# ScalarE's order in a two-FFN decoder step: one copy moved ahead, one cast moved behind, and two loads swapped

## The chip, the cores and the metric

One core of a Trainium2 chip runs the whole step in one launch. The metric is the device time in microseconds; three runs of the kernel before gave a median of 1117.8 us (1117.29 to 1119.15).

Engine names as in the profile: PE is TensorE (matmul), PEld its weight load, DVE is VectorE, ACT is ScalarE, POOL is GpSimd, SP is SyncE, which here only issues DMA loads.

## The reference

One inference step of one decoder layer, in float32, for 512 prompt tokens and 8 x 8 sample tokens, which the kernel treats as 576 columns of one matrix `x`:

```python
x = x + 0.5 * swiglu(rmsnorm(x, ffn1_norm), w_gate, w_up, w_down)   # 1024 -> 2816 -> 1024
h = rmsnorm(x, mix_norm); proj = h @ w_in                          # RG-LRU heads and pooling heads
x = x + concat(y_lru, y_pool) @ w_out
x = x + cross_attend(rmsnorm(x, xattn_norm), mem_k, mem_v, wq, wo)  # 4 heads, 256 memory tokens
x = x + 0.5 * swiglu(rmsnorm(x, ffn2_norm), ...)
y = rmsnorm(x, final_norm)                                         # plus new states, keys and values
```

Prompt tokens attend to keys computed here; each group of sample tokens has its own cached keys (`cache_mem_k`).

## The kernel before

**Arithmetic.** Every operand of a large matmul is kept as two parts: `split` makes a high part with an ACT cast and the low part, the rest, with a DVE subtraction (`wh_`/`wl_` for weights, `dh`/`dl` for weights of the way down, `ph`/`pl` for hidden values). A product is three matmuls: high by high, high by low, low by high.

The larger part of both FFNs, and the query projection, use a scheme with seven block products in place of eight. Weights and activations are cut in 2 x 2 blocks; the products are called 11, E, 22, F, G, 12 and H after the weight block or sum of blocks that they use, and T1 to T4 are sums of activation blocks ("the fourth sum" is T4). The weights come from HBM raw; DVE and POOL's accumulating DMAs form the sums, and `parts_of` or `prepare_22` splits them. `prepare_g` forms the sums for G and F and casts both with one instruction: this is *block G's cast*, `wh_g`.

**The loop of an FFN.** In `ffn`, the loop over `f` handles one chunk of 128 hidden columns: products 11, E, (product 22 of the chunk before, in `finish_chunk`), F, G, 12, H, each of 12 matmuls of 288 columns. Two of these products share a PSUM bank `U`: 11 starts it and F adds to it; then H adds, and 22. Between them ACT must have copied the bank: `out_[0] = s.copy(u2, U)` behind F is *block F's copy*. `u2` goes into the gate, `g`, then Silu (L860) and the up part, `e`; from pairs of chunks `build_a` and `build_b` make the hidden operand (in `build_b`, for odd chunks, the fourth sum's cast).

**The way down.** For the first 16 chunks the product with `w_down` uses the same scheme, in `quick`: for each group of four chunks (`f` = 4, 8, 12, 16) four times the six steps s11, sE, sF, s12, sH and (sG, s22), each of 6 matmuls. These steps are put between the products of the loop: `fill()` stands at seven places in each chunk and runs one step. So the 24 steps of a group run through the chunks with a shift: the fill just behind block F's copy runs s11 in chunks 4, 8, 12, 16, sE in the next chunk, sF in the one after, s12 in the fourth. Each step's result is copied out of PSUM by ACT: s11 and sF with `s.copy` into the banks A (L643, `dA<-dU`) and D (L658, `dD<-dU`), the others with `take` (L636, `add<-...`), which halves it for an accumulating DMA on POOL into `x`. `taken[0]` is the last of these. `ensure` prepares the step's weights (`td` to `dh`, `dl`), `fetch_pair` loads them.

**The order.** PE runs the matmuls as written. On every other engine a planner sets the order when the kernel is built, from the program's order, its own estimate of each duration, and the free buffers. `after_(i, j)` adds an edge without a semaphore: `i` is placed behind `j`. Every engine, and each DMA queue, then runs in its fixed order: what waits holds up all behind it.

**Buffers.** Raw weights use six buffers of one tag, `wr`; a load on SP waits until a buffer's last reader is done. High and low parts have four each, `dh` and `dl` three each.

**The query stage.** `query(p)`, for p = 0 to 3, runs the seven products for two of the eight 128-column blocks of q. In between, `sample_scores(j)` multiplies the sample queries with the cached keys, loaded by `load_keys(j)` (two loads of 512 KB into `wr`), and `load_q(p)` loads raw query weights (also two of 512 KB), used by `prepare_q`, whose additions POOL does for p > 0. Before, `query(p)` calls `load_q(p + 2)` first, and `load_keys(2 * p - 2)` behind `sample_scores(2 * p - 1)`; the scores of block 2p - 2 follow later in the same query.

Of the kernel before, what the change touches and what calls it, by code (L numbers as in the profile page):

```python
# [11 lines left out]
AF = mybir.ActivationFunctionType  # L12
# [57 lines left out]
def hybrid_step(ctx, tc, a):  # L70
# [70 lines left out]
    def after_(i, j):  # L141

        tc.add_manual_dep(i.ins, j.ins.name, mybir.DependencyInfo(
            mybir.DependencyClass.NoSync, mybir.DependencyReason.DATA), reason="order")
# [43 lines left out]
    def split(hi, lo, src, scale=None):  # L188

        if scale is None:  # L190
            i = cast[0] = s.copy(hi, src)  # L191
            if first[0] is not None:
                after_(i, first[0])
            return v.tensor_tensor(out=lo, in0=src, in1=f(hi), op=ALU.subtract)  # L194
        s.activation(hi, src, AF.Copy, scale=scale)
        return v.scalar_tensor_tensor(out=lo, in0=src, scalar=scale, in1=f(hi), op0=ALU.mult, op1=ALU.subtract)
# [171 lines left out]
    def ffn(name, n, fp, turn, plain, head=False):  # L368
# [53 lines left out]
        def parts_of(src, nm_):  # L422
            w = [wp.tile([P, 2, KP, P], F32R, tag=tag, name=f"{tag}_{nm_}") for tag in ("wh", "wl")]
            split(*w, src)
            if out_[0] is not None and nm_ == "e":
                after_(cast[0], out_[0])
            return [lambda q, k, i=i: w[q][:, i, k, :] for i in range(2)]
# [34 lines left out]
        def prepare_g(f):  # L462
            if f < FFC:
                r0, r1 = raws[f]
                v.tensor_add(r0[:, 1], r0[:, 1], r0[:, 0])
                v.tensor_add(r0[:, 0], r0[:, 1], r1[:, 0])  # L466
                W[f]["G"], W[f]["F"] = parts_of(r0, "g")

        def prepare_h(f):
            if f < FFC:  # L470
# [91 lines left out]
        def build_b(p):  # L562
            (hi, lo), b2 = pairs[p], raw[2 * p + 1]
            b21 = b2[:, :HT]
            split(hi[:, N21:N22 + 1, :], lo[:, N21:N22 + 1, :], halves(b2), -1.0)
            v.tensor_sub(b21, b21, t2[p])  # L566
            split(hi[:, T4, :], lo[:, T4, :], b21)

        def build_plain(f):
            if f // 2 not in pairs:  # L570
# [1 line left out]
            split(*hidden(f), raw[f])  # L572

        draw, dparts, made, taken = {}, {}, [0], [None]

        td = fp.tile([P, 4, 2, P], F32, name="td")

# [46 lines left out]
        def quick(g):  # L624

            ps = {}

            def put(i, nm_, b, out, start):
                w = dparts.pop((i, nm_))
                for k in range(2):  # L630
                    for m, (qw, qx) in enumerate(((0, 0), (0, 1), (1, 0))):
                        mm(out, lhsT=w[qw][:, k, :], rhs=pairs[2 * g + k][qx][:, b, :],
                           start=start and k == 0 and m == 0, stop=k == 1 and m == 2, skip_group_check=True)

            def take(dst, src, sign):
                taken[0] = s.activation(dst, src, AF.Copy, scale=0.5 * sign)  # L636

            def s11(i):
                ensure(4 * i + 2)
                ps[i] = cols([single("d", q) for q in ("dU", "dC", "dA", "dD")])  # L640
                U, C, A, D = ps[i]
                put(i, "11", N11, U, True)
                s.copy(A, U)  # L643

            def sE(i):
                U, C, A, D = ps[i]
                put(i, "E", T1, C, True)
                t = halves(rows.tile([P, T], F32, tag="acc", bufs=1, name="add_e"))
                take(t[:, 0, :], C, -1)
                take(t[:, 1, :], C, 1)  # L650
                j = 2 * (i % NQ)
                nc.gpsimd.dma_start(x[:, j:j + 2, HT:], t, accum_op=ALU.add)  # L652

            def sF(i):
                ensure(4 * i + 3)
                U, C, A, D = ps[i]
                put(i, "F", T2, U, False)
                s.copy(D, U)  # L658

            def s12(i):  # L660
                U, C, A, D = ps[i]
                put(i, "12", N21, A, False)
                ps[i, 1] = rows.tile([P, T], F32, tag="sq", name="add_1")
                take(ps[i, 1][:, :HT], A, -1)

            def sH(i):
                ensure(4 * i + 4)
                U, C, A, D = ps[i]
                put(i, "H", T3, U, False)
                ps[i, 2] = rows.tile([P, T], F32, tag="sq", name="add_2")  # L670
                take(ps[i, 2][:, HT:], U, 1)

            def sG(i):
                ensure(4 * i + 5)
                U, C, A, D = ps[i]
                put(i, "G", N22, D, False)
                t = ps.pop((i, 1))
                take(t[:, HT:], D, -1)
                nc.gpsimd.dma_start(x[:, 2 * (i % NQ), :], t, accum_op=ALU.add)  # L679

            def s22(i):
                U, C, A, D = ps[i]
                put(i, "22", T4, U, False)
                t = ps.pop((i, 2))
                take(t[:, :HT], U, 1)
                nc.gpsimd.dma_start(x[:, 2 * (i % NQ) + 1, :], t, accum_op=ALU.add)  # L686

            for i in range(g * NQ, (g + 1) * NQ):
                steps.extend([(q, i) for q in qs] for qs in ((s11,), (sE,), (sF,), (s12,), (sH,), (sG, s22)))
# [121 lines left out]
        for f in range(plain, FFC):  # L811
            w = W[f]
            U, C, A = (single(tag, f"p{tag}")[:, :HT] for tag in "uca")
            product(U, w["11"], n, N11, True)
            out_[0] = s.copy(A, U)
            if f == plain:
                if not head:
                    prepare_g(f)
                load_11(f + 2)
            if f == FFC - 5:  # L820
                fetch(0)
            fill()
            product(C, w["E"], n, T1, True)
            e1 = small_tile("e1")
            out_[0] = s.copy(e1, C)  # L825
            prepare_h(f)
            load_12(f + 2)
            if f == plain:
                sum_eh(f + 1)
            if f == 3:  # L830
                build_a(0)
                build_b(0)
            fill()
            if before:
                finish_chunk(before)
                raw[f - 1] = before[2]
                build(f - 1)
            if f == PLAIN[1][0]:
                down(0)
            prepare_e(f + 1)  # L840
            fill()
            if f in range(4, 4 * FAST + 1, 4):
                quick(f // 4 - 1)
            product(U, w["F"], n, T2, False)
            u2 = small_tile("u2")
            out_[0] = s.copy(u2, U)
            prepare_22(f)
            load_22(f + 2)
            fill()
            product(C, w["G"], n, N22, False)  # L850
            g = full_tile("g")
            v.tensor_add(g[:, HT:], C, u2)
            v.tensor_mul(g[:, HT:], g[:, HT:], r[:, HT:])
            sum_eh(f + 2)
            fill()
            if f == plain:
                (n.last if head else n.last_split)(0, ts[0][:, :, 0, :])
            product(A, w["12"], n, N21, False)
            v.tensor_mul(g[:, :HT], A, r[:, :HT])  # L859
            silu = s.activation(g, g, AF.Silu, scale=-1.0)  # L860
            v.tensor_mul(g, g, r)
            fill()
            if taken[0] is not None:
                after_(silu, taken[0])
            product(U, w["H"], n, T3, False)
            v.tensor_add(e1, U, e1)
            v.tensor_mul(g[:, HT:], e1, g[:, HT:])
            if f == plain:
                (n.last if head else n.last_split)(1, ts[1][:, :, 0, :])
            prepare_g(f + 1)  # L870
            load_11(f + 3)
            raw[f] = g
            if f % 2 and f < 4 * FAST:
                build_a(f // 2)
            if f == 3:
                ensure(2)
            fill()
            first[0] = None
            before = w, U, g
# [335 lines left out]
    if True:  # L1215
# [116 lines left out]
        def query(p):  # L1332
# [7 lines left out]
                v.tensor_mul(z[:, :, e, p * ST:(p + 1) * ST], q[:, TP:].rearrange("p (b k) -> p b k", k=ST),  # L1340
                             rs.rearrange("p (b k) -> p b k", k=ST))

            load_q(p + 2)
            product(U, w["11"], nx, N11, True)
            s.copy(q0[:, :HT], U)
            product(B, w["H"], nx, T3, True)
# [1 line left out]
            if p == 0:  # L1348
                for i in range(2):
                    t = late[:, (3 + 2 * i) * HT:(5 + 2 * i) * HT].rearrange("p (a n) -> p a n", a=2)  # L1350
                    nx.last(i, t)
                qq.extend(operand("q", now["r2"]))
            else:
                sample_scores(2 * p - 1)
                load_keys(2 * p - 2)
            prepare_q(p + 1, "h")

            def middle():
# [369 lines left out]
```

## Time and profile before

| | |
|---|---|
| median of three runs | 1117.8 us |
| profiled execution, its own time | 1118.5 us |
| its span, first to last instruction | 1116.6 us |
| busy: PE, DVE, ACT, POOL | 1102.0, 881.7, 689.0, 212.0 us |
| first FFN's loop and last part | about 48 to 390 us |
| query stage | about 555 to 610 us |
| second FFN, up to the last part | about 765 to 1092 us |
| granted TensorE clock, mean | 0.996 |

Rows of the timeline give the start in us from the span's start, the duration in us, engine, line, operation, what is written and read, and, in brackets, how long the engine stood idle before and what ended that. A row of the waits has who waited for whom, then the sum in us, the number of times and the longest. A row by stretches has the length, then busy time (and instructions) of PE, PEld, DVE, ACT and POOL, the clock, the share of the DMA engines and GB/s. Line 148 is the helper of all matmuls, line 191 that of the casts and line 194 that of the low parts, so there the tile's name tells which it is.

### The profile page before, as it was taken

Reading aid. Unit: us, or ns where it says so; the run is one execution under the profiler, and the core shown is the slowest. Engines: PE = TensorE matmul, PEld = TensorE weight load, DVE = VectorE, ACT = ScalarE, POOL = GpSimd, SP = SyncE. Lnnn points to the kernel's source line nnn. Section 1 sums busy time; section 2 is a strip of 40 time slices with the busy share of each in tenths; the row PEclk is TensorE's granted clock in tenths of the full one; section 3 lists DMA queues with packets and bytes.
Section 4 is the critical chain, followed back from the end, with each engine's and each line's share of the span. In section 5 each row is a group of like instructions: output and inputs, shape, how many; then the busy total and the mean of one; then the engine's idle time right before and its main releaser. Section 6 shows DMA issues by size and latency. Waiting matters only on the chain.

```text
span 1116.6 us, 21977 instructions
## 1 busy us (share of the span) xinstructions
PE 1102.0 (99%) x8386; PEld 1082.6 (97%) x8386; DVE 881.7 (79%) x1577; ACT 689.0 (62%) x1293; POOL 212.0 (19%) x247
## 2 busy tenths in 40 slices
PE   9999999999999999999999999999999999999997
PEld 8999999999999999999988879999999999999996
DVE  7899888889865878979865666679888888787754
ACT  8566666665664645786743555456666666666554
POOL 0012222221221034422131000000222222222211
PEclk9999999999999999999999999999999999999998
DMA  9457767776766655577558862243786777777752
GB/s 324 117 132 177 158 156 170 172 169 147 165 140 144 191 154 134 119 216 166 157 184 289 302 210 80 71 104 84 162 184 151 178 177 166 185 160 156 144 111 85
DMA packets 95545, 181.19 MB, mean 162 GB/s; under 512 B 10000, under 2 KB 47888, under 8 KB 95312
## 3 DMA queue, kind: packets, MB, share of 16 engines
q1 hardware_dynamic: 61312, 125.73, 35.4%
q0 software_dynamic: 31472, 51.65, 28.3%
q10 hardware_dynamic: 2656, 2.41, 0.6%
q8 instruction: 65, 1.06, 0.4%
q14 instruction: 40, 0.33, 0.1%
HBM read 141.92 MB, written 13.20 MB: 139 GB/s over the span
## 4 chain that ended last, share of the span: by engine, by line
PE 91%; DMA 3%; DVE 3%; issue 2%; ACT 1%; POOL 0%; POOLq 0%; SPq 0%; DVEq 0%; ACTq 0%
PE pu L148 22%; PE pc L148 10%; PE dU L148 8%; PE pd L148 6%; PE pa L148 5%; PE xo L148 5%; PE wo L148 5%; PE pg L148 4%; PE in_l L148 2%; PE in_p L148 2%; PE in_g L148 2%; PE k L148 2%; PE v L1438 2%; PE dA L148 2%; PE dC L148 2%; PE dD L148 2%
## 5 line engine op out<-in xcount | busy, mean ns | idle before, releaser
L450 POOL DMA_DIRECT2D r<-f_gu x39 | 34.9, 894 | 361.7 <-DVE r L447 197.5
L191 ACT CAST dh<-td 128x512 fp32r<-128x512 f32 x96 | 59.3, 618 | 30.8 <-PE dA L148 10.7
L148 PE MATMUL dU<-ph,dh 128*128 128x288 f32 x256 | 75.7, 296 | 1.2 <-ACT add L636 1.2
L148 PE MATMUL dU<-pl,dh 128*128 128x288 f32 x256 | 75.4, 295 | 0.0
L148 PE MATMUL dU<-ph,dl 128*128 128x288 f32 x256 | 75.4, 295 | 0.0
L194 DVE TENSOR_TENSOR dl<-td,dh 128x512 fp32r<-128x512 f32 x96 | 64.6, 686 | 10.3 <-ACT dh L191 10.2
L194 DVE TENSOR_TENSOR wl_e<-r,wh_e 128x1024 fp32r<-128x1024 f32 x39 | 47.6, 1222 | 28.3 <-ACT wh_e L191 28.3
L652 POOL DMA_DIRECT2D x<-add_e x32 | 38.9, 1214 | 144.6 <-ACT add_e L636 46.8
L191 ACT CAST wh_g<-r 128x1024 fp32r<-128x1024 f32 x39 | 41.0, 1051 | 26.8 <-DVE r L466 13.7
L679 POOL DMA_DIRECT2D x<-add x32 | 31.0, 968 | 136.8 <-ACT add L636 92.5
L194 DVE TENSOR_TENSOR wl_h<-r,wh_h 128x1024 fp32r<-128x1024 f32 x39 | 47.6, 1220 | 3.0 <-ACT wh_h L191 3.0
L148 PEld LDWEIGHTS dU<-ph,dh 128*128 128x128 f32 x256 | 48.1, 188 | 1.6 <-ACT add L636 1.6
L148 PEld LDWEIGHTS dU<-ph,dl 128*128 128x128 f32 x256 | 48.2, 188 | 0.0
L148 PEld LDWEIGHTS dU<-pl,dh 128*128 128x128 f32 x256 | 48.1, 188 | 0.0
L194 DVE TENSOR_TENSOR wl_g<-r,wh_g 128x1024 fp32r<-128x1024 f32 x39 | 47.6, 1222 | 0.3 <-ACT wh_g L191 0.3
L191 ACT CAST wh_h<-r 128x1024 fp32r<-128x1024 f32 x39 | 40.9, 1048 | 10.3 <-PE pu L148 7.2
L191 ACT CAST wh_e<-r 128x1024 fp32r<-128x1024 f32 x39 | 41.1, 1053 | 0.6 <-PE pg L148 0.6
L860 ACT ACTIVATE g<-g 128x576 f32<-128x576 f32 x39 | 26.7, 683 | 23.9 <-DVE g L859 22.3
L686 POOL DMA_DIRECT2D x<-add x32 | 36.9, 1153 | 1.0 <-ACT add L636 0.8
L191 ACT CAST ph<-g 128x576 fp32r<-128x576 f32 (+1 forms) x39 | 22.9, 587 | 18.6 <-DVE g L566 10.5
L825 ACT COPY e<-pc 128x288 f32<-128x288 f32 x39 | 15.6, 401 | 29.1 <-PE pc L148 28.1
L636 ACT ACTIVATE add<-dU 128x288 f32<-128x288 f32 x64 | 26.2, 409 | 11.7 <-PE dU L148 11.7
(649 smaller groups left out, 4650.5 us busy)
## 6 DMA issues: line engine op xcount, KB each, us to landing
x<-add POOLq DMA_DIRECT2D x80, 288.0 KB, 5.7
r<-f_gu SPq DMA_DIRECT2D x39, 512.0 KB, 3.9
r<-f_gu SPq DMA_DIRECT2D x78, 256.0 KB, 3.5
td<-f_d SPq DMA_DIRECT2D x80, 128.0 KB, 4.9
r<-f_gu POOLq DMA_DIRECT2D x39, 256.0 KB, 4.6
x<-add_e POOLq DMA_DIRECT2D x32, 288.0 KB, 4.7
dsum<-f_d POOLq DMA_DIRECT2D x32, 256.0 KB, 4.8
ck<-ck SPq DMA_DIRECT2D x16, 512.0 KB, 4.8
```

Source lines behind the costliest of these rows:

```text
L148: i = te.matmul(*args, **kw)
L191: i = cast[0] = s.copy(hi, src)
L194: return v.tensor_tensor(out=lo, in0=src, in1=f(hi), op=ALU.subtract)
L450: nc.gpsimd.dma_start(r0[:, 0], wgu[f - plain, :, 3], accum_op=ALU.add)
L636: taken[0] = s.activation(dst, src, AF.Copy, scale=0.5 * sign)
L652: nc.gpsimd.dma_start(x[:, j:j + 2, HT:], t, accum_op=ALU.add)
L679: nc.gpsimd.dma_start(x[:, 2 * (i % NQ), :], t, accum_op=ALU.add)
L686: nc.gpsimd.dma_start(x[:, 2 * (i % NQ) + 1, :], t, accum_op=ALU.add)
L825: out_[0] = s.copy(e1, C)
L860: silu = s.activation(g, g, AF.Silu, scale=-1.0)
L1438: te.matmul(ps[:, m, :HD], lhsT=lhs[:, kd, ms], rhs=w[wi][:, k, :], start=kd == 0 and i == 0, stop=kd == DC - 1 and i == 2)
```

## The change

Four edits of order; no instruction is added or removed.

- Block F's copy (`u2`) is noted in `due`, and the next copy of the way down in the program's order (a `take`, or the copy of s11 or sF) gets an edge behind it.
- The fourth sum's cast, noted in `fourth` by `build_b`, gets an edge behind block F's copy of the same chunk.
- Block G's cast for the next chunk gets an edge behind the last `take` written ahead of it.
- In `query(p)` for p > 0, `load_keys(2 * p - 2)` is the first call and `load_q(p + 2)` comes behind `sample_scores(2 * p - 1)`; `query(0)` still begins with `load_q(2)`.

```diff
 prepare_g
                 W[f]["G"], W[f]["F"] = parts_of(r0, "g")
+                if taken[0] is not None:
+                    after_(cast[0], taken[0])
 build_b
             split(hi[:, T4, :], lo[:, T4, :], b21)
+            fourth[0] = cast[0]
+        due, fourth = [None], [None]
+
+        def behind_due(i):
+            if due[0] is not None:
+                after_(i, due[0])
+                due[0] = None
+            return i
 quick
             def take(dst, src, sign):
-                taken[0] = s.activation(dst, src, AF.Copy, scale=0.5 * sign)
+                taken[0] = behind_due(s.activation(dst, src, AF.Copy, scale=0.5 * sign))
 s11
-                s.copy(A, U)
+                behind_due(s.copy(A, U))
 sF
-                s.copy(D, U)
+                behind_due(s.copy(D, U))
 the loop over f
             u2 = small_tile("u2")
-            out_[0] = s.copy(u2, U)
+            out_[0] = due[0] = s.copy(u2, U)
+            if fourth[0] is not None:
+                after_(fourth[0], out_[0])
+                fourth[0] = None
             prepare_22(f)
 query
-            load_q(p + 2)
+            if p:
+                load_keys(2 * p - 2)
+            else:
+                load_q(2)
             product(U, w["11"], nx, N11, True)
...
                 sample_scores(2 * p - 1)
-                load_keys(2 * p - 2)
+                load_q(p + 2)
```

## The prediction

> **What bounds the kernel now.** I read the page first, then busy time by stretches, then the waits of TensorE, and last the timeline around each wait.
>
> ```profile
> PE 1102.0 (99%) x8386; PEld 1082.6 (97%) x8386; DVE 881.7 (79%) x1577; ACT 689.0 (62%) x1293; POOL 212.0 (19%) x247
> ```
> ```profile
> 60.00:127.00 67.00, 65.84 (x497) 65.57 (x496) 61.03 (x112) 46.83 (x94) 15.52 (x16) 1.00 0.69 159
> ...
> 765.00:1092.00 327.00, 327.00 (x2462) 327.00 (x2461) 263.66 (x458) 211.33 (x431) 69.78 (x73) 1.00 0.70 158
> ```
> ```profile
> PE dU L148 <- ACT add L636: 1.2, 2, 0.8
> PE pu L148 <- ACT u L846: 1.2, 1, 1.2
> PE ss L148 <- DMA ck<-ck: 0.9, 2, 0.5
> PE pu L148 <- DVE e L866: 0.3, 1, 0.3
> ```
>
> TensorE (PE) is the bound: 1102.0 of 1116.6 us busy. No number of matmuls changes, so the change can only give back idle time of PE, 14.6 us in all with start and tail. The second FFN (765 to 1092) has none: 327.00 of 327.00. There the change can only stay neutral or lose. In the first FFN and the query stage the view of waits names the places: two waits for a copy of the way down ("add", L636), one for block F's copy (u, L846), two for keys (ck). The fourth row, VectorE's e, is not touched.
>
> **The change part by part: block F's copy (u2) ahead.** PE and ScalarE (ACT) around 69 us, in block f=4:
>
> ```profile
> 69.08 0.29 PE L148 MATMUL dU<-ph,dl 128*128 128x288 f32 x1
> 70.53 0.40 PE L148 MATMUL pu<-n1h,wh_h 128*128 128x288 f32 x1 [1.16 <-ACT u L846]
> 70.77 0.30 PE L148 MATMUL pu<-n1l,wh_h 128*128 128x288 f32 x1
> ```
> ```profile
> 65.23 0.39 ACT L643 COPY dA<-dU 128x288 f32<-128x288 f32 x1
> 66.61 0.62 ACT L191 CAST dh<-td 128x512 fp32r<-128x512 f32 x1 [0.99 <-DVE td L617]
> ...
> 69.75 0.43 ACT L191 CAST ph<-g 128x288 fp32r<-128x288 f32 x1
> 70.09 0.39 ACT L846 COPY u<-pu 128x288 f32<-128x288 f32 x1
> ```
>
> Product F ended before 65.23, yet its copy ran at 70.09, behind the way down's dA copy, a cast that waited for VectorE (DVE), and the fourth sum's cast (ph<-g, 69.75). H writes the same bank and stood still. The new edges put u2 ahead of exactly these: it runs near 65.2 and the others 0.39 us later. H needs it at 69.2 (69.08 plus one step of 0.13); the product that reads dA comes only behind H's twelve steps, 1.6 us later, and the fourth sum is needed later still, so their delay is hidden by H. A running step is 0.13 us; here two steps took 70.77 - 69.08 = 1.69, so the stall costs 1.69 - 0.26 = 1.43 us, of which 0.27 is the restart behind the wait of 1.16. The same pair stands in block f=16:
>
> ```profile
> 272.35 0.29 PE L148 MATMUL dU<-ph,dl 128*128 128x288 f32 x1
> 272.68 0.40 PE L148 MATMUL pu<-n1h,wh_h 128*128 128x288 f32 x1
> ```
>
> 0.33 - 0.13 plus about 0.1 of restart: 0.30. In every other block u2 already ends ahead of H, so its edges cost and bring nothing.
>
> **Block G's cast behind the copies.** The place in block f=15; the same happens at 189 us (f=11):
>
> ```profile
> 257.02 0.29 PE L148 MATMUL dD<-ph,dl 128*128 128x288 f32 x1
> 258.08 0.40 PE L148 MATMUL dU<-ph,dh 128*128 128x288 f32 x1 [0.77 <-ACT add L636]
> 258.31 0.29 PE L148 MATMUL dU<-pl,dh 128*128 128x288 f32 x1
> ```
> ```profile
> 256.67 1.05 ACT L191 CAST wh_g<-r 128x1024 fp32r<-128x1024 f32 x1 [2.85 <-DVE r L466]
> 257.62 0.40 ACT L636 ACTIVATE add<-dU 128x288 f32<-128x288 f32 x1
> ```
>
> ACT sat 2.85 us on the cast wh_g, which waited for DVE's sum, while the copy of dU behind it was ready. PE's last fast product needs that bank. Removed: 1.29 - 0.26 = 1.03 us here; at 189 us the waits' row leaves 1.2 - 0.8 = 0.4, with the same 0.26 of restart 0.66.
>
> What it costs: wh_g goes behind the copies in 16 blocks of each FFN. The furthest move is in every fourth block (f = 7, 11, 15, 19), best seen in the second FFN:
>
> ```profile
> 835.77 1.05 ACT L191 CAST wh_g<-r 128x1024 fp32r<-128x1024 f32 x1 [0.47 <-PE pc L148]
> ...
> 840.16 0.40 ACT L636 ACTIVATE add<-dU 128x288 f32<-128x288 f32 x1
> ```
> ```profile
> L860 ACT ACTIVATE g<-g 128x576 f32<-128x576 f32 x39 | 26.7, 683 | 23.9 <-DVE g L859 22.3
> ...
> L194 DVE TENSOR_TENSOR wl_g<-r,wh_g 128x1024 fp32r<-128x1024 f32 x39 | 47.6, 1222 | 0.3 <-ACT wh_g L191 0.3
> ```
> ```profile
> 846.02 0.29 PE L148 MATMUL pu<-n2h,wh_g 128*128 128x288 f32 x1
> ```
>
> From 835.77 to 840.56 the cast moves by 4.8 us. With 0.68 for the Silu that stands there (third column of the two grouped rows: mean ns of one), 1.05 for itself and 1.22 for DVE's low half, the weights are ready near 843.5; PE reads them at 846.02. Slack 2.5 us: the three products between hide it on PE. What is queued behind: DVE's low half frees a raw buffer, so SP's load of raw weights, and behind it on SP the loads of the way down's weights, start up to 4.8 us later; POOL's accumulating load follows those. Between gain and loss I take no PE time for this in the second FFN. In the first, DVE has little slack:
>
> ```profile
> 78.65 0.68 DVE L194 TENSOR_TENSOR dl<-td,dh 128x512 fp32r<-128x512 f32 x1
> ```
> ```profile
> 80.17 0.30 PE L148 MATMUL dU<-ph,dh 128*128 128x288 f32 x1
> ```
> ```profile
> DVE td L608 <- DMA td<-f_d: 25.9, 9, 5.3
> ```
> ```profile
> 194.45 0.45 DVE L866 TENSOR_TENSOR e<-pu,e 128x288 f32<-128x288 f32 x1
> ```
> ```profile
> 195.94 0.29 PE L148 MATMUL pu<-n1h,wh 128*128 128x288 f32 x1
> ```
>
> DVE is busy 61.03 of 67 us in the first stretch. With PE 1.43 us earlier, the product at 80.17 would want, two steps on (79.00), a half that DVE finishes at 79.33: 0.33 us lost, I charge 0.3 (bounds 0 and 0.33). Later, product 22 at 195.94 overwrites a bank that DVE reads until 194.90: slack 1.04 us. wh_g's low half, 1.22 us of DVE, leaves its place ahead of that read, but DVE also waits 25.9 us in all for way-down weights, which may now come later. By the second such block PE is 1.13 + 0.66 + 1.03 = 2.8 us earlier. Bounds for both blocks together: nothing lost, or the two stalls of 1.69 us given back whole; I charge 0.5, nearer to nothing, since the 1.22 us leave.
>
> **Keys ahead of raw query weights.**
>
> ```profile
> 568.94 1.86 SPq L1309 DMA_DIRECT2D q<-wqs  x2
> 570.90 11.27 SPq L1293 DMA_DIRECT2D ck<-ck  x5
> ```
> ```profile
> 577.17 0.29 PE L148 MATMUL qb<-nxh,wl_q 128*128 128x288 f32 x1
> ...
> 579.56 0.40 PE L148 MATMUL qc<-nxh,wh_qG 128*128 128x288 f32 x1
> ```
> ```profile
> 584.29 0.29 PE L148 MATMUL qb<-nxh,wl_qH 128*128 128x288 f32 x1
> ...
> 585.52 0.40 PE L148 MATMUL qu<-nxh,wh_qF 128*128 128x288 f32 x1
> ```
> ```profile
> DMA to landing us min/median/max: 3.5/4.8/7.6
> ```
>
> Disturbed, the keys' scores take 579.56 - 577.17 = 2.39 us, undisturbed 585.52 - 584.29 = 1.23: 1.16 us to gain. Two key loads swap with two weight loads on SP, in query 1 alone (later queries have no weights left to load). They then start at 568.94 and 570.47, and even with the longest 7.6 us land at 576.5 and 578.1, against a need near 577.4 (577.17 plus the 0.2 of the change of shape) and, for the second key tile, half of the 1 us of scores later, 577.9: at most 0.2 us stays. I take 1.16. The weights' pair starts from 570.9, about 2 and 1 us later. Who waits for it:
>
> ```profile
> 572.72 1.44 POOL L1326 TENSOR_TENSOR q<-q 128x512 f32<-128x512 f32 x1 [4.93 <-DMA q<-wqs]
> ```
> ```profile
> 577.03 1.05 ACT L191 CAST wh_qF<-q 128x1024 fp32r<-128x1024 f32 x1 [3.89 <-POOL q L1321]
> ```
>
> POOL's add on them stands ahead of the adds for the next query's F, and ACT's cast wh_qF waited 3.89 us for POOL. If POOL keeps this order and the weights land 7.6 us after 571, all of it moves 6 us: wh_qF from 577.0 to 583, its low half ready near 585.4, and F (584.4 by then) waits up to 0.8 us. The Trainium skill, "DMA: Bandwidth & Descriptors", section "Anatomy of one DMA", fits about 2.0 us plus bytes over 436 GB/s, an estimate of 3.2 us for 512 KB; by that F never waits and this part is worth the full 1.16, by the longest row 0.36. The fit is for POOL's own path and the quickest row here, 3.5 us, lies above it.
>
> **Sum.** 1.43 + 0.30 + 1.03 + 0.66 + 1.16 = 4.58 us, less 0.3 and 0.5: 3.8. The profiled execution took 1118.5 us (span 1116.6), so 1114.7 by its own time; it stood 0.7 above the median, so 1114.0 against 1117.8.
>
> **Rivals.** *DVE and its loads set the pace of the first FFN.* Speaking for it: 61.03 of 67 us busy and 25.9 us of waits for td; against: PE loses nothing from 765 to 1092 with the same order, though there DVE has no L608. Then what ACT gives back is lost elsewhere, and the keys' 1.16 stay: 1116.6.
>
> *Slower.* Block G's low half comes late in the second FFN: it decides from the point where the cast or DVE behind it slips 2.5 us beyond my 843.5, by SP's later loads blocking DVE in order. At 1 us in each of the eight such blocks of both FFNs, 8 us: 1117.8 - 4.6 + 8 = 1121.2. Against: ACT is busy only 211.33 of 327.
>
> *The edges don't do it.* An edge fixes one pair; the planner that writes each engine's order sets the rest anew. If another cast that waits for DVE then stands ahead of u2 or of the copies, as the three different ones at 66.61, 69.75 and 256.67 do now, the same stalls come back under other names: about 1117.8, no change. Against: each edge names the very instruction that stood in the way.
>
> **How the numbers follow.** About 0.2% (2.2 us) is what a measurement can tell here. Forecast as told 0.60; DVE's pace 0.18, of which 0.03 reaches 2.2 us; no change 0.09; slower 0.13. Faster 0.63, same 0.24, slower 0.13. The range runs from the full sum with the runs' lower spread of 0.5 (1112.7) to no change with the same spread (1118.3): about 0.05 lies below it and 0.11 above. The forecast's own range is 1112.7 to 1115.6.
>
> **What would show it.** Right: no wait of PE for u, add or ck; u2 before the dA copy in f=4 and f=16; wh_g behind the last add in f=11 and f=15; ck ahead of q on SP near 569 us; 765 to 1092 shorter by nothing. Wrong: a new PE wait on wl_g or on DVE L866, longer waits of DVE L608 for td, PE under 327 of 327 in the second FFN, or PE waiting at wh_qF near 584 us.

## The result, and the profile after

The changed kernel took 1128.4 us (median of five runs, 1127.17 to 1128.77); the kernel before, run beside it, 1118.4. The ratio is 1.0076, 95% interval [1.0061, 1.0090]: slower by 8.5 us (10.0 between the two medians), where 3.8 us of gain was forecast. The profiled execution took 1127.4 us, with a span of 1125.1 against 1116.6, again 8.5.

The waits of TensorE:

```profile
PE dU L148 <- ACT dA L653: 7.2, 7, 2.3
...
PE dU L148 <- ACT add L646: 0.6, 1, 0.6
...
PE pu L148 <- DVE e L879: 0.3, 1, 0.3
```

The waits for u and for the keys are gone, those for "add" have shrunk from 0.8 + 0.4 to 0.6. In their place stands one that was not there: seven waits for the dA copy, 7.2 us. In block f=4, ScalarE and then VectorE in the changed kernel's timeline:

```profile
65.08 0.62 ACT L191 CAST dh<-td 128x512 fp32r<-128x512 f32 x1
66.97 0.62 ACT L191 CAST dh<-td 128x512 fp32r<-128x512 f32 x1 [1.28 <-DVE td L627]
67.50 0.68 ACT L195 ACTIVATE ph<-g 128x576 fp32r<-128x576 f32 x1
70.19 0.40 ACT L856 COPY u<-pu 128x288 f32<-128x288 f32 x1 [2.01 <-DVE g L568]
70.48 0.43 ACT L191 CAST ph<-g 128x288 fp32r<-128x288 f32 x1
70.82 0.40 ACT L653 COPY dA<-dU 128x288 f32<-128x288 f32 x1
```
```profile
69.02 0.68 DVE L194 TENSOR_TENSOR wl<-r,wh 128x512 fp32r<-128x512 f32 x1
69.63 0.45 DVE L568 TENSOR_TENSOR g<-g,t 128x288 f32<-128x288 f32 x1
```

u2 did not run near 65.2. It waited until 70.19 for L568, VectorE's subtraction of `t2` for the fourth sum, although u2 has nothing to do with that value. The tie is a buffer:

```python
def small_tile(nm_):
    return fp.tile([P, HT], F32, tag="pc", bufs=2, name=nm_)
...
t2[p] = small_tile("t2")          # build_a, end of an odd chunk
e1 = small_tile("e1")             # next chunk
u2 = small_tile("u2")             # next chunk: takes t2's buffer
...
v.tensor_sub(b21, b21, t2[p])     # build_b (L568), t2's last reader
```

With two buffers, u2 of an even chunk overwrites t2 and must wait for its last reader. So it was before as well (there L566 began at 69.26 and u2 at 70.09). The edge added the rest: the dA copy, at 65.23 before, had to stand behind u2 and ran at 70.82. TensorE's next step of the way down, sF, adds into the bank that this copy reads:

```profile
68.65 0.29 PE L148 MATMUL pa<-n1h,wl_h 128*128 128x288 f32 x1
71.27 0.61 PE L148 MATMUL dU<-ph,dh 128*128 128x288 f32 x1 [2.33 <-ACT dA L653]
71.68 0.45 PE L148 MATMUL dU<-pl,dh 128*128 128x288 f32 x1
```

The step behind the wait is 0.41 us and those that follow 0.24 instead of 0.13. By stretches, the 3.1 us behind four of the waits, and a stretch without one (74.60) between:

```profile
71.30:74.40 3.10, 3.10 (x13) 3.10 (x14) 3.06 (x8) 1.27 (x4) 2.07 (x2) 0.50 0.57 111
74.60:77.70 3.10, 3.10 (x25) 3.10 (x25) 3.07 (x6) 2.99 (x6) 0.00 (x0) 1.00 1.04 205
140.90:144.00 3.10, 3.10 (x24) 3.10 (x25) 3.10 (x8) 2.98 (x7) 1.21 (x1) 1.00 0.51 105
211.20:214.30 3.10, 3.10 (x15) 3.10 (x14) 2.82 (x5) 2.03 (x4) 1.24 (x1) 0.50 0.60 122
280.20:283.30 3.10, 3.10 (x24) 3.10 (x25) 3.10 (x8) 2.97 (x7) 1.23 (x1) 1.00 0.55 117
```

PE counts as fully busy in all five and yet does 13 or 15 matmuls instead of 24 or 25: the clock fell to half behind two of the waits, a second price of about 1.5 us each (the 9 to 12 missing matmuls, at 0.13, are 1.2 to 1.6).

Both traces have the same 8386 matmuls in the same order, so the start of the k-th in one can be set against the start of the k-th in the other. How far the changed kernel lags:

| where (time after) | lag, us | what came in |
|---|---|---|
| before 68 | 0.4 | the start |
| 74.6, f=4 | 3.0 | wait for dA +2.5, half clock and restart +1.6, the u stall gone -1.4 |
| 140.8, f=8 | 4.2 | dA +1.2 |
| 194.8, f=11 | 4.5 | "add" +0.3 |
| 214.4, f=12 | 8.0 | dA +1.9, half clock and restart +1.6 |
| 265.2, f=15 | 7.1 | "add" -0.9 |
| 280.1, f=16 | 8.4 | dA +1.2 |
| 281.1, f=16 | 8.2 | the u stall gone -0.3 |
| 586.2, keys | 7.2 | +0.1 at 341 us, keys -0.5 and -0.7 |
| 994.6, second FFN | 8.7 | dA three times +0.5 |

### The profile page after: what moved, and what is told of

It reads as the page before. It is cut to its first block, busy times and chain, and to the rows that moved or that the text cites. A ratio compares the mean times of both kernels' runs of the same rounds, so it can differ in the third digit from the quotient of the medians.

```text
span 1125.1 us, 21955 instructions
## 1 busy us (share of the span) xinstructions
PE 1105.8 (98%) x8386; PEld 1085.5 (96%) x8386; DVE 881.6 (78%) x1577; ACT 686.1 (61%) x1293; POOL 209.8 (19%) x247
## 4 chain that ended last, share of the span: by engine, by line
PE 84%; DVE 8%; DMA 3%; issue 3%; ACT 1%; SPq 0%; POOL 0%; POOLq 0%; DVEq 0%; ACTq 0%
PE pu L148 18%; PE pc L148 8%; PE dU L148 8%; PE pd L148 6%; PE xo L148 5%; PE wo L148 5%; PE pa L148 4%; PE pg L148 3%; PE in_l L148 2%; PE in_p L148 2%; PE in_g L148 2%; PE k L148 2%; PE v L1454 2%; DMA td<-f_d 2%; PE dA L148 2%
## 5 line engine op out<-in xcount | busy, mean ns | idle before, releaser
L689 POOL DMA_DIRECT2D x<-add x32 | 29.3, 917 | 174.0 <-ACT add L646 138.6
L856 ACT COPY u<-pu 128x288 f32<-128x288 f32 x39 | 15.6, 400 | 42.9 <-DVE g L568 19.6
L447 DVE TENSOR_TENSOR r<-r 128x512 f32<-128x512 f32 x39 | 26.8, 688 | 18.9 <-DMA r<-f_gu 18.9
L874 DVE TENSOR_TENSOR g<-g,rstd_n 128x576 f32<-128x576 f32 x39 | 29.4, 755 | 8.5 <-ACT g L873 8.3
```

Source lines behind the costliest of these rows:

```text
L447: i = v.tensor_add(r1[:, 1], r0[:, 0], r0[:, 1])
L856: out_[0] = due[0] = s.copy(u2, U)
```

## The experiments

**Theory 1**: u2 waits for t2's buffer, and the edge hands this wait to the dA copy and so to sF. **Theory 2**: block G's cast, moved behind the copies, makes VectorE late, and its fourth sum with it. **Theory 3**: VectorE and its loads set the pace of the first FFN, whatever is reordered on ScalarE. Each kernel was timed against the kernel before on the same chip (1119.3 to 1119.6 us there).

**Which edge: taken out, and alone.** The kernel without the `due` edge:

```diff
         def behind_due(i):
             if due[0] is not None:
-                after_(i, due[0])
                 due[0] = None
```

> The changed kernel without the one edge that puts the copies of the way down behind u2; the fourth sum's cast behind u2, block G's cast behind the copies and the keys stay. Theory 1 (u2 shares its buffer with t2 and runs only behind VectorE's fourth sum, so the edge carries that wait to the dA copy): no wait of PE for ACT dA, no half clock, u2 still behind g L568; 1115.5 to 1117.5. Theory 2 (block G's late cast delays VectorE, so that its fourth sum is late): the time stays above 1122. Theory 3 (VectorE and its loads set the pace of the first FFN): 1117.2, the keys alone.

1118.5 us, ratio 0.9990 [0.9981, 1.0000]. No wait for dA is left and the clock is 0.997. The loss is gone, against theory 2; the time is 1 us above the top of theory 1's span, and u2 still waits for the buffer, now with three waits of TensorE behind it in place of one.

```profile
PE pu L148 <- ACT u L855: 1.4, 3, 0.8
```

The `due` edge alone, the three other edits undone:

> The kernel before with only that edge: each way-down copy behind u2. Theory 1: the whole loss and more, since neither keys (1.2) nor block G's cast (0.9 near 257 us) give back: 1118.4 + 8.7 + 2.1 = about 1129, with waits of PE for ACT dA of about 2 us in f=4, 8, 12, 16 and the half clock behind the longest of them. Theory 2: no loss, 1118.4 within 1.

1127.2 us, ratio 1.0071 [1.0058, 1.0084]. This one edge makes the loss, the half clock behind its longest wait included:

```profile
PE dU L148 <- ACT dA L651: 4.4, 4, 2.2
PE dU L148 <- ACT add L644: 2.0, 3, 0.8
```

It shows four waits, not seven: none in the second FFN. The kernel with everything but block G's edge:

```diff
                 W[f]["G"], W[f]["F"] = parts_of(r0, "g")
-                if taken[0] is not None:
-                    after_(cast[0], taken[0])
```

> The changed kernel without the edge on block G's cast (edges on u2 and the keys stay). Theory 1: the loss stays, since it sits in the dA copy behind u2: 1126 to 1129, with waits for ACT dA near 7 us. Theory 2 (block G's cast behind the copies makes VectorE late): the loss goes, 1118 to 1119. Between them: what the cast adds to the loss through VectorE.

1125.1 us, ratio 1.0057 [1.0045, 1.0069]; 5.3 us of waits for dA, again four, and 327.00 of 327.00 us in the second FFN (326.11 with the edge):

```profile
PE dU L148 <- ACT dA L651: 5.3, 4, 2.3
```

So the loss stays without block G's edge; with it come the three small waits of the second FFN (1.5 us), which neither edge has alone, and, at f=12, an idle time of 1.75 us in place of 0.89, which was followed by the half clock. The two intervals of the ratio overlap, so this share of theory 2 is seen in one profiled execution of each and not in the times.

**The two parts by themselves.** The keys' swap alone (the diff's part in `query`):

> The kernel before with the swap of key loads and raw query weights alone. Every theory: the stall of the keys' scores near 577 us goes and nothing else moves. Measured inside the changed kernel this part gave 0.52 + 0.68 = 1.2 us, so 1117.2 against 1118.4. If it is 0, the gain seen inside the changed kernel came from the later arrival of PE there, not from the loads.

1117.4 us, ratio 0.9984 [0.9975, 0.9992]; in the trace the scores gain 0.46 and 0.68 us, matmul by matmul, close to the forecast 1.16. This kernel also shows how far a single wait scatters. Up to the query stage its order on ScalarE, VectorE and GpSimd is that of the kernel before, and yet in f=12 TensorE waits for u2, which it did not before, and lags 0.6 us more behind it:

```profile
205.63 0.40 PE L148 MATMUL pu<-n1h,wh_h 128*128 128x288 f32 x1 [0.35 <-ACT u L846]
```

A difference of that size between two traces says little by itself.

Block G's edge alone:

> The kernel before with only block G's cast behind the way down's copies. My prediction's terms: 1.03 + 0.66 less charges of 0.5, so 1117.2 and no new wait in the second FFN. Theory 2: 1122 or more, with u2 and the fourth sum later than before. Theory 3: 1118.4.

1119.5 us, ratio 0.9993 [0.9984, 1.0003]: no change that can be told. In its trace the stalls at 258 and 190 us give back 1.03 and 0.67 us (1.03 and 0.66 forecast). Other places take as much: the start +0.65, u2 in f=8 and f=12 +0.36 and +0.27, the keys' scores +0.57. Whether the edge causes any of these, one trace can't tell; theory 2's 1122 is excluded.

**The buffer, first try.** If the shared buffer is the cause, t2 in another place frees u2. The pair's first `g` tile is spent by then and free for two more chunks:

```diff
-            t2[p] = small_tile("t2")
+            t2[p] = b11
...
-            v.tensor_sub(t2[p], b22, b11)
             v.tensor_sub(b12, b12, b22)
             split(hi[:, T1:T3 + 1:2, :], lo[:, T1:T3 + 1:2, :], t)
-            split(hi[:, T2, :], lo[:, T2, :], t2[p])
+            v.tensor_sub(b11, b22, b11)
+            split(hi[:, T2, :], lo[:, T2, :], b11)
```

With all the change's edits:

> The changed kernel, but t2 is written into the first half of the pair's spent g tile (free until block 2p+3) instead of the two-buffer tag that it shares with e1 and u2; sums and casts are the same, VectorE's subtraction for t2 comes behind the T1, T3 split. Theory 1 (shared buffer): u2 runs as soon as product F has ended, near 65.5 us, no wait of PE for ACT dA or u, no half clock; against the kernel before 1.43 + 0.30 (u2), 0.73 + 0.43 (block G, as measured alone) and 1.2 to 1.5 (keys) are gained: 4.1 to 4.4 us, so 1115.1 to 1115.4 against 1119.5. Rival (VectorE's late fourth sum holds PE in another way, or the edge is costly in itself): the waits for dA stay, 1125 or more. Rival (VectorE sets the pace of the first FFN): keys alone, 1117.5 to 1118.

1121.0 us, ratio 1.0014 [1.0003, 1.0024]. Half a hit: no wait for dA or u is left, but the gain did not come. A new wait stands near 229 us (in a profiled execution that was the slowest of twelve, 1123.9 us):

```profile
PE dU L148 <- ACT add L646: 3.1, 2, 2.5
```
```profile
225.07 0.62 ACT L191 CAST dh<-td 128x512 fp32r<-128x512 f32 x1 [5.05 <-DVE td L619]
...
228.73 0.40 ACT L646 ACTIVATE add<-dU 128x288 f32<-128x288 f32 x1
```
```profile
224.10 0.42 DVE L618 TENSOR_TENSOR td<-td 128x256 f32<-128x256 f32 x1 [3.50 <-DMA td<-f_d]
```

VectorE stood 3.5 us on a load of way-down weights, ScalarE's cast 5.0 us on VectorE, and the copy that PE needed stood behind it. The three others of this group:

> The kernel before with only t2 moved out of u2's buffer. Theory 1: u2 is free to run early but the order on ScalarE is the planner's; if it now comes ahead of the dA copy without an edge, the stall of 1.43 near 69 us goes and the time is 1117 to 1118; if not, 1119.5. Never slower by over 0.5.

1123.1 us, ratio 1.0033 [1.0020, 1.0046]: a clear miss, slower by 3.7 where at most 0.5 was allowed. The stall at 70 us went (-1.4), but there are five waits for "add", 5.4 us together, in place of two with 1.2. The three longest stand where block G's cast waits ahead of the copy, as at 258 us in the kernel before, after VectorE waited 5.0 to 5.2 us for a load of way-down weights. The first of the three:

```profile
118.10 0.43 DVE L608 TENSOR_TENSOR td<-td 128x256 f32<-128x256 f32 x1 [5.00 <-DMA td<-f_d]
```
```profile
122.84 1.04 ACT L191 CAST wh_g<-r 128x1024 fp32r<-128x1024 f32 x1 [2.85 <-DVE r L466]
123.80 0.40 ACT L636 ACTIVATE add<-dU 128x288 f32<-128x288 f32 x1
```

> As the kernel with every edge and t2 moved, without the edge on block G's cast. Theory: it lacks the 0.73 + 0.43 near 257 and 189 us, so 1 us longer than that one: 1116.2 to 1116.5. If block G's late cast costs VectorE something hidden, it is the quicker of the two.

1121.9 us, ratio 1.0023 [1.0015, 1.0032]: over 5 us above the expected time, and not told apart from the kernel with the edge, whose interval overlaps.

> As the kernel with every edge and t2 moved, without the edge that puts the way down's copies behind u2. Theory: with the buffer free the edge has little left to do, since the planner can place u2 at F's end; within 0.5 us of the kernel with it, 1115 to 1116. If the edge is what brings u2 ahead, u2 stays behind the dA copy and up to 1.7 us are missing: 1117.

1121.0 us, ratio 1.0016 [1.0007, 1.0026]: 5 us above the expected time, but the same as with the `due` edge. Once the buffer is free, that edge no longer hurts and no longer helps. But the moved subtraction changes VectorE's order too, so this group tells the buffer's part from theory 3 badly. Theory 3 has a part in it: the longest new waits lead back to loads for VectorE. Why the loads come later under that order was not tried.

**The buffer, second try.** u2 instead of t2 is moved: into the first half of the chunk's own `g` tile, taken one product earlier. VectorE's sums stay as they are.

```diff
-            u2 = small_tile("u2")
+            g = full_tile("g")
+            u2 = g[:, :HT]
...
             product(C, w["G"], n, N22, False)
-            g = full_tile("g")
```

With all edits:

> The changed kernel with u2 written into the first half of the block's own g tile (taken one product earlier) instead of the buffer shared with t2; VectorE's sums keep their order. Theory 1: no wait of PE for ACT dA or u, u2 near 64 to 65.5 us, no half clock from those. If the long waits for 'add' near 190 to 262 us, seen with t2 moved, came from the moved subtraction, they are gone and the time is 1115 to 1116; if they come from VectorE's waits for way-down weights (td) under the new order, they stay and the time is 1119 to 1121.

1116.2 us, ratio 0.9974 [0.9964, 0.9984]: the same four edits, 0.76% slower before, are now 0.26% faster. u2 (written as g) and the dA copy in f=4, in the order that the prediction wanted:

```profile
63.96 0.39 ACT L857 COPY g<-pu 128x288 f32<-128x288 f32 x1
64.30 0.62 ACT L191 CAST dh<-td 128x512 fp32r<-128x512 f32 x1
64.82 0.62 ACT L191 CAST wh<-r 128x512 fp32r<-128x512 f32 x1
65.34 0.39 ACT L653 COPY dA<-dU 128x288 f32<-128x288 f32 x1
```

One long wait is left, by the same chain as near 229 us above (load of td, VectorE, ScalarE's cast, the copy behind it), with the half clock behind it in this profiled execution (1118.7 us, near the top of its runs, 1114.6 to 1119.2):

```profile
121.59 0.43 DVE L618 TENSOR_TENSOR td<-td 128x256 f32<-128x256 f32 x1 [3.18 <-DMA td<-f_d]
123.03 0.62 ACT L191 CAST dh<-td 128x512 fp32r<-128x512 f32 x1 [5.77 <-DVE td L619]
124.32 0.40 PE L148 MATMUL dU<-ph,dh 128*128 128x288 f32 x1 [1.92 <-ACT add L646]
```

Then with the keys and block G's edge only, neither of the edges that name u2:

> The kernel before with u2 in g, block G's cast behind the copies, and the keys' swap; none of the edges that name u2. Theory 1: the two edges on u2 have little to do once its buffer is free, so within 0.7 us of the kernel with all edges and u2 in g, and no wait for dA or u.

1115.4 us, ratio 0.9978 [0.9968, 0.9989].

> The kernel before with u2 in g and the keys' swap, no edge. The keys give 1.5 to 2 us as measured alone; the u stall of 1.43 near 69 us goes as well: 1116 against 1119.5. If longer waits for 'add' behind block G's cast come up, as when t2 was moved in the kernel before (five, 5.4 us together), it is 1121.

1116.5 us, ratio 0.9979 [0.9970, 0.9988]. The three intervals overlap and all lie below 1; what the three share is u2's own buffer and the keys. The keys alone gave 0.9984 [0.9975, 0.9992], which overlaps with them: what the buffer adds to the kernel before is seen in the traces, where the u stall is gone, and not in the times, and u2 in g was not run without the keys. What the times do show is the changed kernel with and without it, 1.0076 against 0.9974. The edges on u2 are not needed: with the buffer free, the planner itself puts u2 at 64.70, ahead of the dA copy at 66.10 (kernel with the keys and block G's edge):

```profile
64.70 0.40 ACT L856 COPY g<-pu 128x288 f32<-128x288 f32 x1
...
66.10 0.39 ACT L652 COPY dA<-dU 128x288 f32<-128x288 f32 x1
```

That kernel's stretches of the first and the second FFN, against 65.84 and 327.00 before:

```profile
60.00:127.00 67.00, 66.76 (x503) 66.45 (x503) 61.89 (x114) 46.65 (x94) 15.51 (x16) 1.00 0.69 161
...
765.00:1092.00 327.00, 327.00 (x2464) 326.86 (x2462) 260.35 (x455) 210.09 (x430) 69.80 (x73) 1.00 0.70 156
```

## Why the prediction was wrong, by its own steps

**The step that failed** is "it runs near 65.2 and the others 0.39 us later". It was read from the order on ScalarE: what stood ahead of u2 was taken for what held it. In a queue that runs in order, a row without an idle time of its own may have been held as well, by something that ended while the engine was busy. In the kernel before:

```profile
69.26 0.46 DVE L566 TENSOR_TENSOR g<-g,t 128x288 f32<-128x288 f32 x1
69.41 0.38 ACT L658 COPY dD<-dU 128x288 f32<-128x288 f32 x1 [0.70 <-PE dU L148]
```

The fourth sum's cast (69.75) and u2 (70.09) both needed L566, which ended at 69.72. Neither row has a bracket, since ScalarE was at the dD copy until 69.79. That u2 and t2 share two buffers is in the code and was not weighed. In f=16, taken for "the same pair", the kernel before shows the wait itself: the dA copy was long done, ScalarE stood idle for L566, and u2 followed:

```profile
269.71 0.39 ACT L643 COPY dA<-dU 128x288 f32<-128x288 f32 x1
271.89 0.43 ACT L191 CAST ph<-g 128x288 fp32r<-128x288 f32 x1 [1.79 <-DVE g L566]
272.23 0.39 ACT L846 COPY u<-pu 128x288 f32<-128x288 f32 x1
```

**The second step that failed** is "their delay is hidden by H": the product that reads dA does come behind H, but sF, six steps ahead of H, writes the bank that the dA copy reads. The delayed copy was needed ahead of the row at 71.27 shown above, which without the stall would have stood at 68.65 + 0.13 = 68.8, not behind H. With u2 at 65.2 and 0.39 us of delay this would have cost nothing, so the first step decides; but it turned a useless edge into a loss.

**What was not in the sum at all**: the half clock, twice, about 1.5 us each.

**The stalls were sized right.** In the kernel with u2 in g, the keys and block G's edge, the stalls went as the prediction told it. Its gain (a loss with a minus), matmul by matmul against the kernel before:

| term | forecast | measured |
|---|---|---|
| u stall in f=4 | 1.43 | 1.43 |
| u stall in f=16 | 0.30 | 0.31 |
| "add", f=15 | 1.03 | 1.03 |
| "add", f=11 | 0.66 | 0.67 |
| keys | 1.16 | 1.17 |
| charge: dl, f=5 | -0.3 | -0.51 |
| charge: 22 behind VectorE's e | -0.5 | 0 |
| small losses at 226 and 330 us | none | -0.29 |
| sum | 3.78 | 3.8 |

So the stalls were sized well, and the edit was not the one that removes them. That the sums agree so closely is in part luck: one charge of 0.5 did not come, and 0.5 of other losses did. The charge for dl went past its bound of 0.33, since the wait, which delayed the matmul by 0.40, came with a restart of 0.11:

```profile
79.92 0.40 PE L148 MATMUL dU<-ph,dl 128*128 128x288 f32 x1 [0.24 <-DVE dl L194]
```

That kernel's span is 3.5 us shorter than before (1113.1 against 1116.6); the rest, +0.3, is at the start and the tail. The profiled execution was the quickest of its twelve (1114.9 to 1120.0); by the ratio the gain is 1.2 to 3.6 us.

**Keys and the weights' lateness.** For F near 584 the prediction weighed 0.36 us (longest row) against the full 1.16 (by the fit of the Trainium skill, "DMA: Bandwidth & Descriptors", section "Anatomy of one DMA"). F never waited, but not because the weights were quick: POOL did not keep its order. In the changed kernel the addition on the swapped weights, L1339, stands behind the one that F's cast needs, L1334:

```profile
582.75 1.39 POOL L1334 TENSOR_TENSOR q<-q 128x512 f32<-128x512 f32 x1
586.27 1.34 POOL L1339 TENSOR_TENSOR q<-q 128x512 f32<-128x512 f32 x1 [2.14 <-DMA q<-wqs]
```

It began 7.1 us behind the first issue of that pair (579.20), near the longest row's 7.6. The fit's estimate of 3.2 us lies far below that.

**The rivals.** That DVE sets the pace did not decide, though the longest waits of TensorE led back to its waits for td wherever t2 was moved, and in the profiled execution of the kernel with all edges and u2 in g. "Slower" was foreseen by block G's low half; no wait on it came, but one of the signs named for being wrong did, PE under 327 of 327 in the second FFN (326.11), by the dA copy. "The edges don't do it" came nearest: u2 was not freed. But it expected the old stalls under new names, not that an edge makes a second instruction wait for what the first one waits for.

## What to carry to other kernels

An order edge passes on every wait of the instruction it names. Before putting B behind A, find out what A itself waits for, buffers included: the last readers of whatever had its buffer before, not only what stands ahead of it in the queue; then look for the first reader or writer on any engine that needs B. Where A is late because of a buffer, give it another buffer first; here the planner's own order then did what the edges were meant to do.

## What the runs showed of the hardware

A wait of TensorE can have a second price. In the loops of the first FFN, over all profiled kernels here, none of the idle times up to 1.65 us was followed by a lower clock, and all seven from 1.75 us on were (1.75, 1.92, 2.25, 2.32, 2.33, 2.48 and 2.81). The longest without and one behind 1.92 us:

```profile
193.20 0.40 PE L148 MATMUL dU<-ph,dh 128*128 128x288 f32 x1 [1.65 <-ACT add L636]
```
```profile
193.30:196.80 3.50, 3.50 (x27) 3.50 (x28) 3.46 (x8) 2.83 (x7) 1.81 (x2) 1.00 0.29 39
```
```profile
124.32 0.40 PE L148 MATMUL dU<-ph,dh 128*128 128x288 f32 x1 [1.92 <-ACT add L646]
...
125.15 0.44 PE L148 MATMUL dU<-ph,dl 128*128 128x288 f32 x1
...
128.03 0.44 PE L148 MATMUL pu<-n1h,wl_h 128*128 128x288 f32 x1
```

The steps of 0.24 us run from 125.15 to 128.27, and in the seven cases begin between 0 and 1.5 us behind the restart and go on for 2.6 to 3.1 us. In the changed kernel the trace's records of the granted clock have half from 71.105 to 74.518 and from 211.051 to 214.464, 3.413 us each. In all traces the changes of the clock lie whole multiples of 3.413 us apart. PE was idle for 1.75 to 2.57 us of the stretch of 3.413 us just before each of the seven falls, and for at most 1.65 us of any other such stretch in these loops.

The length of one wait is not the whole rule. In the first kernel with t2 moved, outside these loops, the clock fell behind a wait of 0.92 us, which was followed by ten matmuls of a single column:

```profile
546.55 1.28 PE L148 MATMUL k<-ones,acc_nx 128*128 128x1 f32 x10 [0.92 <-ACT t_nx L1296]
```
```profile
548.00:551.40 3.40, 3.40 (x18) 3.40 (x17) 2.53 (x7) 1.26 (x3) 0.41 (x1) 0.50 0.29 71
```

The Trainium skill, "TensorE: Matmul & The Clock Gate", section "Part 1: The HAM clock gate", describes half rate until about 3.4 us of sustained work; that length agrees. It has the clock fall after an idle window of about 3.4 us, and here 1.75 us was enough.
